# Strassen's seven products for both output projections of a two-layer encoder

## Chip, cores and metric

The kernel runs on one core of a Trainium2 chip. The metric is the device time of one execution in microseconds, as a median over runs of the same kernel. The core's engines are TensorE (PE, matmuls), VectorE (DVE), ScalarE (ACT), GpSimd (POOL) and SyncE (SP, which only issues DMAs here).

## What is computed

The encoder has two layers on 1024 tokens of width 1024. Layer 0 mixes tokens by neighbourhood attention, layer 1 by grouped-query attention with rotary positions. Around each mixer the reference does the same:

```python
for i in range(DEPTH):                       # DEPTH = 2
    h = rms_norm(x, norm_g[i])
    y = mixer(h, ...)                        # (o * silu(gate)) @ w_out is its last step
    x = x + y
    g = jax.nn.sigmoid(rms_norm(x, ple_norm_g[i]) @ ple_w_gate[i])
    x = x + g * (p[i] @ ple_w_proj[i])
return rms_norm(x, final_norm_g)
```

The change is in the product with `w_out`: (1024 x 1024) @ (1024 x 1024), once per layer.

## The kernel before

Each layer is a mixer (`mixer_a`, `mixer_b`) and then `dense_phase(l)`, which holds the output projection ("out") and the gate ("ple"). All products are done in about float32 precision with operands split in two: a high part, rounded to the matmul's type, and a low part, the rest. `split3` adds high by high, high by low and low by high into one PSUM bank, so every 128 x 128 by 128 x 512 product is three matmuls, recorded at line 315.

The left operand, the mixer's output, lies transposed in two resident tiles `HTh` and `HTl` (high and low; eight token tiles t of 128, eight contraction steps k of 128). During the mixer a head pair's output is split by `split` in `head_end` and stored to DRAM, and `load_y` brings it back into `HTh` and `HTl` near the mixer's end. The last pair (k = 7) is written by `fin_last` directly.

The right operand comes in units of 128 x 1024 floats (512 KB). The class `Weights` (`WQ`) goes through a list of units in order: `stage` loads a unit into one of two staging slots (`wstage`), `pump` splits it (high part on ACT at line 225, low part on DVE at line 230) into a pool with a limit of live units (`cap`), `get` forces it, `done` frees it, and `hold` names a unit at which loading stops. `pump` is called once after each piece of matmul work.

In `dense_phase` the projection's loops run over two halves of 512 output columns and eight token tiles, with eight k each: 16 groups of 24 matmuls, each in a PSUM bank of its own, added into the residual `X[t]` by DVE (line 1286). For the first four tiles all k below 4 come first. While the second half runs, finished tiles are normalised: ACT squares (lines 1360, 1369), `norm_r` with eleven small DVE instructions, a scaling on DVE (line 1382), and `to_ht` (PE transposes, ACT copy to `HTh` at 444, DVE rest to `HTl` at 445), placed three steps later between the projection's matmuls by `pend_ht`. The gate's two halves follow in the same way, with a tanh on ACT and two DVE instructions per tile (`gated`). In layer 0 `rope_tables`, which needs POOL, DVE and DMAs on SP, is run after tile 4 of the projection's first half.

Every engine takes its instructions in program order; the order between engines is set by semaphores. The program order is written out by hand.

## Time and profile before

| | us |
|---|---|
| median of 3 runs | 1548.74 |
| lowest, highest | 1548.33, 1549.39 |
| span of the profiled execution | 1548.4 |
| first matmul of the output projection, layer 0 and layer 1, from the start of the span | 529.28, 1355.76 |

The profile gives no time of its own for the profiled execution beside its span, first to last instruction; the span lies within the range of the runs. A row of a timeline reads: start, duration, engine, line, operation, output<-input, shapes, and in brackets how long the engine was idle before and which instruction ended that. A group's row reads: count, total busy time and mean ns of one, then the idle time before. PE's durations overlap, since matmuls are pipelined: the pitch from start to start is what counts.

### The profile page before, as it was taken

What the parts mean: (1) busy time and instruction counts of PE and PEld (TensorE: products, weight loads), DVE (VectorE), ACT (ScalarE), POOL (GpSimd) and SP (SyncE); (2) the same over time, 40 slices, a digit from 0 to 9 for tenths busy, and PEclk for the clock granted to TensorE, in tenths of its full rate; (3) what the DMA queues carried; (4) which work ended last, traced back from release to release, by engine and by line L of the source; (5) the groups of instructions that cost most, each with busy time, mean ns of one, the idle gap of its engine ahead of it and who ended that gap; (6) DMA issues with size and microseconds to landing.
All of it is one profiled execution on the core that took longest, in us unless ns stands there. A gap on an engine that the chain in (4) does not pass through costs nothing.

```text
span 1548.4 us, 24286 instructions
## 1 busy us (share of the span) xinstructions
PE 1521.1 (98%) x9072; PEld 1328.5 (86%) x9072; DVE 1016.2 (66%) x1990; ACT 874.1 (56%) x1757; POOL 280.4 (18%) x380
## 2 busy tenths in 40 slices
PE   8999999999999999999999999999999999999997
PEld 8888988988988888888988889989999888788886
DVE  7666576576477436557877776777777877625636
ACT  6565465465466522333567776767767767622422
POOL 1221121121121010000312122444131200000022
PEclk9999999999999999999999999999999999999999
DMA  8212122122033961232210111111101123651213
GB/s 263 97 40 72 60 80 61 52 82 79 35 99 97 355 232 55 79 139 78 75 48 22 38 48 50 41 38 56 57 27 42 62 62 116 224 197 55 74 54 131
DMA packets 90005, 138.32 MB, mean 89 GB/s; under 512 B 17056, under 2 KB 56096, under 8 KB 89888
## 3 DMA queue, kind: packets, MB, share of 16 engines
q1 hardware_dynamic: 87296, 129.17, 25.6%
q10 hardware_dynamic: 2592, 7.61, 1.4%
q8 instruction: 71, 1.16, 0.3%
q14 instruction: 46, 0.38, 0.1%
HBM read 104.13 MB, written 36.15 MB: 91 GB/s over the span
## 4 chain that ended last, share of the span: by engine, by line
PE 41%; DVE 7%; ACT 3%; issue 2%; DMA 0%; SPq 0%; ACTq 0%; DVEq 0%
PE d L315 22%; PE o L315 7%; PE t L1144 6%; PE s L315 5%; DVE PTl L1147 2%; DVE mn L1128 1%; ACT PTh L1146 1%; ACT P L1134 1%; PE t L443 1%; DVE QS L1108 1%; DVE wl L230 0%; PE t L1098 0%; DVE t L962 0%; DVE qt L963 0%; DVE Y L459 0%
## 5 line engine op out<-in xcount | busy, mean ns | idle before, releaser
L315 PE MATMUL d<-wh,HTh 128*128 128x256 f32 (+1 forms) x1096 | 369.3, 339 | 3.6 <-ACT HTh L444 1.3
L315 PE MATMUL d<-wh,HTl 128*128 128x256 f32 (+1 forms) x1096 | 363.2, 333 | 0.3 <-DVE HTl L445 0.3
L315 PE MATMUL d<-wl,HTh 128*128 128x256 f32 (+1 forms) x1096 | 362.6, 333 | 0.0
L1147 DVE TENSOR_TENSOR PTl<-t,PTh 128x512 fp32r<-128x512 f32 x256 | 164.4, 684 | 110.1 <-ACT PTh L1146 109.7
L315 PEld LDWEIGHTS d<-wh,HTh 128*128 128x128 f32 x1096 | 206.4, 189 | 26.6 <-ACT HTh L444 1.6
L315 PEld LDWEIGHTS d<-wl,HTh 128*128 128x128 f32 x1096 | 206.7, 189 | 21.7
L315 PEld LDWEIGHTS d<-wh,HTl 128*128 128x128 f32 x1096 | 206.5, 189 | 22.0 <-DVE HTl L445 0.5
L315 PE MATMUL d<-HTh,wh 128*128 128x512 f32 x504 | 205.8, 408 | 0.0
L315 PE MATMUL d<-HTh,wl 128*128 128x512 f32 x504 | 198.1, 393 | 0.0
L315 PE MATMUL d<-HTl,wh 128*128 128x512 f32 x504 | 197.5, 392 | 0.0
L1134 ACT ACTIVATE P<-s,mn 128x1024 f32<-128x1024 f32 x128 | 142.8, 1115 | 57.2 <-DVE mn L1128 56.3
L1146 ACT ACTIVATE PTh<-t 128x512 fp32r<-128x512 f32 x256 | 140.2, 594 | 45.4 <-PE t L1144 44.8
L1128 DVE TENSOR_REDUCE mn<-s 128x1 f32<-128x1024 f32 x128 | 154.8, 1209 | 11.7 <-PE s L315 11.6
L1144 PE MATMUL t<-ident,P 128*128 128x128 f32 x1024 | 137.7, 275 | 6.4 <-DVE PTl L1147 4.4
L230 DVE TENSOR_TENSOR wl<-wstage,wh 128x1024 fp32r<-128x1024 f32 x86 | 110.2, 1285 | 40.1 <-ACT wh L225 39.6
L1144 PEld LDWEIGHTS t<-ident,P 128*128 128x128 f32 x1024 | 114.6, 140 | 22.5 <-DVE PTl L1147 16.6
L315 PE MATMUL s<-KA,QS 128*128 128x512 f32 (+2 forms) x384 | 133.5, 402 | 0.0
L315 PE MATMUL s<-KB,QS 128*128 128x512 f32 (+2 forms) x384 | 121.7, 371 | 0.0
L315 PE MATMUL o<-PTh,V 128*128 128x256 f32 (+2 forms) x672 | 118.8, 288 | 1.2 <-DVE Y L459 0.9
L315 PE MATMUL o<-PTl,V 128*128 128x256 f32 (+2 forms) x672 | 119.0, 288 | 0.1
L695 DVE TENSOR_TENSOR PTl<-t,PTh 128x384 fp32r<-128x384 f32 (+1 forms) x128 | 66.6, 520 | 74.7 <-ACT PTh L694 73.4
L315 PEld LDWEIGHTS d<-HTh,wl 128*128 128x128 f32 x504 | 94.6, 188 | 21.7
(201 smaller groups left out, 2486.0 us busy)
## 6 DMA issues: line engine op xcount, KB each, us to landing
wstage<-in_wts SPq DMA_DIRECT2D x92, 512.0 KB
pp<-ppD SPq DMA_DIRECT2D x32, 256.0 KB
X<-in_x SPq DMA_DIRECT2D x15, 512.0 KB
rb<-rD SPq DMA_DIRECT2D x56, 128.0 KB
ppD<-th SPq DMA_DIRECT2D x20, 256.0 KB
xD<-X SPq DMA_DIRECT2D x8, 512.0 KB
X<-xD SPq DMA_DIRECT2D x8, 512.0 KB
yD0h<-rb SPq DMA_DIRECT2D x14, 256.0 KB
```

The costliest lines, as they stand in the source:

```text
L230: eng.tensor_tensor(lo[:, c:c + n], s[:, c:c + n], hi[:, c:c + n], ALU.subtract)
L315: pe.matmul(ps, a, b, start=first, stop=last, skip_group_check=True)
L443: pe.transpose(ps[:, k], xn[:, (4 * c + k) * 128:(4 * c + k + 1) * 128], ident)
L695: dve.tensor_tensor(PTl[:, sl], ps[:, :m], PTh[:, sl], ALU.subtract)
L1108: post.add(DQ, lambda: dve.tensor_tensor(qs[oth], raw[own], qs[own], ALU.subtract))
L1128: dve.tensor_reduce(mn, ps, axis=AX.X, op=ALU.min)
L1134: act.activation(p, ps, AF.Exp, bias=mn, scale=-1.0, accum_out=RS[h, hf][:, t:t + 1])
L1144: pe.transpose(ps[:, i], p[:, k * 128:(k + 1) * 128], ident)
L1146: act.activation(PTh[:, ks, c], ps, AF.Copy)
L1147: dve.tensor_tensor(PTl[:, ks, c], ps, PTh[:, ks, c], ALU.subtract)
```

## The change

Both operands of the projection are cut in halves: A (the mixer's output) by tokens and contraction into A11, A12, A21, A22, B (the weights) by contraction and columns. A quarter of A is four token tiles by four k. A block is one token tile of one product: four k, 12 matmuls into one bank. There are seven products of four blocks, in this order: A11 B11 (blocks 0 to 3), A12 B21 (4 to 7), S2 T2 (8 to 11), S3 T3 (12 to 15), A22 T4 (16 to 19), and, mixed, S1 T1 and Q4 B22 (20 to 27). The sums of A are S1 = A21 - A22, S2 = S1 - A11, S3 = A11 - A21, Q4 = S2 + A12; those of B are T3 = B22 + B12, T2 = T3 + B11, T4 = T2 + B21, T1 = B11 + B12. Products three to five and the last one add into the bank that an earlier product left (`start` False), after DVE's `fold` has read it.

The sums are made on chip while the blocks run. A dictionary `todo` gives each block a function that is issued after it. The sums of B need raw units in the staging slots and two more tiles (`sum0`, `sum1`); 14 raw units are loaded per layer beside the four that `WQ` splits, 18 where there were 8. DVE makes T3, POOL T2, T4 and T1; S1 and S2 are made by POOL for tiles 0, 2 and 3, by DVE for tile 1; S3 and Q4 by DVE. All sums are then split by ACT (high) and DVE (low), those of A back into `HTh` and `HTl`.

The mixers store A21's columns of the first four head pairs unsplit. The normalisation between projection and gate now squares whole rows on ACT, has its small instructions per pair of tiles (m, 4 + m), and the gate's first half goes through the tiles in the order 0, 4, 1, 5, 2, 6, 3, 7. The gate's weights are loaded only from block 20 on (`hold`). `rope_tables` comes after the last tile of the gate's first half.

```diff
-        for n in ("out", "ple"):
-            for hf in range(2):
-                q.extend([((n, l, hf, u), 1 + hf) for u in range(4)])
+        q.extend([(("out", l, 0, u), 1) for u in range(4)])
+        q.extend([(("ple", l, 0, u), 1) for u in range(4)])
+        q.extend([(("ple", l, 1, u), 4 - u // 2 * 2) for u in range(4)])
...
+    def strassen_out(l, X, ps_d, ps_t):
...
+        def halves(name, u, pid, src):
+            def hi():
+                if u == 0:
+                    W[name] = [None, None]
+                W[name][u] = WQ.alloc[pid]()
+                act.activation(W[name][u][0], src(), AF.Copy)
+
+            def lo():
+                w = W[name][u]
+                dve.tensor_tensor(w[1], src(), w[0], ALU.subtract)
+            return hi, lo
...
+        def s12(eng, m):
+            S1[m], S2[m] = piece("S1", 4), piece("S2", 2)
+            eng.tensor_tensor(S1[m], a21(m), h(4 + m, 1), ALU.subtract)
+            eng.tensor_tensor(S1[m], S1[m], lw(4 + m, 1), ALU.subtract)
+            eng.tensor_tensor(S2[m], S1[m], h(m, 0), ALU.subtract)
+            eng.tensor_tensor(S2[m], S2[m], lw(m, 0), ALU.subtract)
+
+        def s3(m):
+            S3[m] = piece("S3", 2)
+            dve.tensor_tensor(S3[m], h(m, 0), a21(m), ALU.subtract)
+            dve.tensor_tensor(S3[m], S3[m], lw(m, 0), ALU.add)
+
+        def q4(m):
+            Q4[m] = piece("Q4", 4)
+            dve.tensor_tensor(Q4[m], S2[m], h(m, 1), ALU.add)
+            dve.tensor_tensor(Q4[m], Q4[m], lw(m, 1), ALU.add)
...
+        def total(eng, u, dst, a, b):
+            eng.tensor_tensor(dst, a, b, ALU.add)
+
+        for u in range(2):
+            load(tc_[u], q22[u])
+            fetch(u, q12[u])
+        for t in range(2):
+            sync.dma_start(X[t], xs[t])
...
+        def f0():
+            s12(pool, 0)
+            for t in (2, 3):
+                sync.dma_start(X[t], xs[t])
+        at(0, f0)
+        def f1():
+            total(dve, 0, tc_[0], tc_[0], raw[0])
+            fetch(0, q11[0])
+            s3(0)
+        at(1, f1)
+        def f2():
+            total(dve, 1, tc_[1], tc_[1], raw[1])
+            fetch(1, q11[1])
+            s12(dve, 1)
+            s3(1)
+        at(2, f2)
+        def f3():
+            total(pool, 0, raw[0], raw[0], tc_[0])
+            hi_s(S2, 0)
+            hi_s(S3, 0)
+            lo_s(S2, 0)
+            lo_s(S3, 0)
+            q4(0)
+        at(3, f3)
+        def f4():
+            total(pool, 1, raw[1], raw[1], tc_[1])
+            hi_w("t3", 0)()
+            hi_s(S2, 1)
+            hi_s(S3, 1)
+            lo_s(S2, 1)
+            lo_s(S3, 1)
+        at(4, f4)
+        def f5():
+            s12(pool, 2)
+            lo_w("t3", 0)()
+            hi_w("t2", 0)()
+            q4(1)
+            for t in (4, 5):
+                sync.dma_start(X[t], xs[t])
+        at(5, f5)
+        def f6():
+            lo_w("t2", 0)()
+            hi_w("t2", 1)()
+            s3(2)
+        at(6, f6)
+        def f7():
+            s12(pool, 3)
+            lo_w("t2", 1)()
+            hi_w("t3", 1)()
+        at(7, f7)
+        def f8():
+            load(tc_[0], q21[0])
+            hi_s(S2, 2)
+            hi_s(S3, 2)
+            lo_w("t3", 1)()
+            lo_s(S2, 2)
+            lo_s(S3, 2)
+            s3(3)
+            for t in (6, 7):
+                sync.dma_start(X[t], xs[t])
+        at(8, f8)
+        def f9():
+            load(tc_[1], q21[1])
+            q4(2)
+            hi_s(S2, 3)
+            hi_s(S3, 3)
+            lo_s(S2, 3)
+            lo_s(S3, 3)
+        at(9, f9)
+        def f10():
+            total(pool, 0, tc_[0], tc_[0], raw[0])
+            q4(3)
+            fetch(0, q12[0])
+        at(10, f10)
+        def f11():
+            total(pool, 1, tc_[1], tc_[1], raw[1])
+            fetch(1, q12[1])
+        at(11, f11)
+        def first(m):
+            xt = X[m][:, 0:512]
+            pool.tensor_tensor(xt, xt, P1[m], ALU.add)
+        def f12():
+            hi_w("t4", 0)()
+            first(0)
+            first(1)
+        at(12, f12)
+        def f13():
+            lo_w("t4", 0)()
+            hi_w("t4", 1)()
+            load(tc_[0], q11[0])
+            first(2)
+            first(3)
+        at(13, f13)
...
+        def block(ps, t, c, wk, start):
+            for k in range(4):
+                wh, wl = W[wk][k // 2]
+                cc = slice((k % 2) * 512, (k % 2) * 512 + 512)
+                split3(ps, HTh[:, t, 4 * c + k, :], HTl[:, t, 4 * c + k, :], wh[:, cc], wl[:, cc],
+                       start and k == 0, k == 3)
+
+        def fold(t, c, ps, op):
+            xt = X[t][:, 512 * c:512 * c + 512]
+            if op is ALU.subtract:
+                dve.tensor_tensor(xt, xt, ps, op)
+            else:
+                dve.tensor_tensor(xt, ps, xt, op)
...
+        for wk, t0, c, xt0, xc, op in (("t2", 4, 0, 0, 1, ALU.subtract), ("t3", 0, 0, 4, 1, ALU.subtract),
+                                       ("t4", 4, 1, 4, 0, ALU.add)):
+            for m in range(4):
+                block(Y[m], t0 + m, c, wk, False)
+                fold(xt0 + m, xc, Y[m], op)
+                pulse()
+        WQ.live[1] += 2
+        WQ.live[2] += 2
+        for kind, m in ((5, 0), (5, 1), (3, 0), (5, 2), (3, 1), (5, 3), (3, 2), (3, 3)):
+            if kind == 5:
+                Y[m] = ps_d.tile([128, 512], F32, name="d")
+                block(Y[m], m, 1, "t1", True)
+                fold(4 + m, 1, Y[m], ALU.add)
+            else:
+                block(Y[m], 4 + m, 0, "b22", False)
+                fold(m, 1, Y[m], ALU.add)
+            pulse()
+            if clock[0] == 21:
+                es.close()
+            if (kind, m) == (5, 3):
+                WQ.live[1] -= 2
+            if (kind, m) == (3, 3):
+                WQ.live[2] -= 2
+            yield kind, m
...
+            for n, (step, m) in enumerate(strassen_out(l, X, ps_d, ps_t)):
...
+                if step == 5:
+                    act.activation(junk, X[4 + m], AF.Square, accum_out=ss[:, 2 * m + 1:2 * m + 2])
+                else:
+                    act.activation(junk, X[m], AF.Square, accum_out=ss[:, 2 * m:2 * m + 1])
+                    sm = ss[:, 2 * m:2 * m + 2]
+                    r = sb.tile([128, 2], F32, name="rn", bufs=4)
+                    wk = sb.tile([128, 8], F32, name="wkn", bufs=2)
+                    dve.tensor_scalar(sm, sm, 0.5 / D, 0.5 * EPS, op0=ALU.mult, op1=ALU.add)
+                    rsqrt(r, sm, wk)
+                    ready.append(((m, 4 + m), r))
+                WQ.pump()
+                pend_ht()
+                scale_pair()
```

More of the change, by code (lines that the diff above doesn't have):

```diff
@@ L256, in trunk @@
     WQ = Weights()
-    WQ.hold = ("bg", 0)
+    WQ.hold = ("ple", 0, 0, 0)
     q = WQ.q
@@ L530, in fin @@
             pool.tensor_tensor(Y, Y, rb, ALU.mult)
-            post.add(YS[layer], split)
+            if pair < 4 and hf == 1:
+                post.add(YS[layer] + 2, lambda: store(0, Y))
+            else:
+                post.add(YS[layer], split)
         return fin_last if pair == 7 else fin
@@ L1176, in mixer_b @@
                 if not pend:
-                    WQ.hold = None
+                    WQ.hold = ("ple", 1, 0, 0)
                 d[0]()
@@ L1263, in pend_ht, with scale_pair @@
                     to_ht(ps_t, *pend.pop(0)[1:])
-            for kind in ("out", "ple"):
-                final = kind == "ple" and l == 1
+            ready = []
+            def scale_pair():
+                if not ready or len(pend) > 4:
+                    return
+                ts, r = ready.pop(0)
+                xs = []
+                for i, t in enumerate(ts):
+                    xn = xalloc()
+                    dve.scalar_tensor_tensor(xn, X[t], r[:, i:i + 1], g1, op0=ALU.mult, op1=ALU.mult)
+                    xs.append(xn)
+                pend.extend([(clock[0] + 3, t, xn, (c,)) for c in range(2) for t, xn in zip(ts, xs)])
@@ L1267, in dense_phase @@
+            WQ.age, WQ.lag = age, lag
+            for kind in ("ple",):
+                final = l == 1
                 sq = sb.tile([128, 2, NT], F32, name="sq")
-                gt = g1 if kind == "out" else g2
+                gt = g2
                 for hf in range(2):
@@ L1329, in last_tile, with load_pp @@
                         WQ.done(*keys)
-                    def load_pp(t):
-                        if kind == "ple" and t < NT:
-                            PP[t] = sb.tile([128, 512], F32, name="pp")
-                            sync.dma_start(PP[t], ppD[l][t, :, cs])
-                    order = [(t, i) for t in range(NT) for i in range(2)]
-                    if kind == "out" and hf == 0:
-                        order = [(t, 0) for t in range(4)] + [(t, 1) for t in range(4)] + order[8:]
+                    def load_pp(i):
+                        if i < NT:
+                            PP[seq[i]] = sb.tile([128, 512], F32, name="pp")
+                            sync.dma_start(PP[seq[i]], ppD[l][seq[i], :, cs])
+                    order = [(t, i) for t in seq for i in range(2)]
+                    if hf == 0:
+                        order = [(t, i) for p in range(4) for i in range(2) for t in seq[2 * p:2 * p + 2]]
                     if final and hf == 1:
@@ L1342, in dense_phase @@
                     for t, i in order:
-                        if kind == "out" and hf == 0 and i == 0:
-                            sync.dma_start(X[t], xs[t])
                         if final and hf == 1 and t == NT - 1:
```

161 lines of the change are left out of this document (138 added, 23 removed).

## The prediction

> **What bounds the kernel now.** I read the page first, then the chain that ended last, then the windows around both output projections, then the timelines of PE, DVE, POOL and SP there and the groups by shape for durations.
>
> ```profile
> span 1548.4 us, 24286 instructions
> PE 1521.1 (98%) x9072; PEld 1328.5 (86%) x9072; DVE 1016.2 (66%) x1990; ACT 874.1 (56%) x1757; POOL 280.4 (18%) x380
> ...
> 1355.76 63.42 PE d L315 x276
> ```
>
> ```profile
> 536.00:587.00 51.00, 51.00 (x225) 41.90 (x224) 17.14 (x25) 13.05 (x26) 5.50 (x4) 1.00 0.65 219
> 1358.00:1415.00 57.00, 57.00 (x251) 46.85 (x250) 16.02 (x29) 12.99 (x26) 0.00 (x0) 1.00 0.40 148
> 595.00:635.00 40.00, 40.00 (x202) 32.77 (x201) 29.57 (x62) 14.72 (x29) 0.00 (x0) 1.00 0.19 57
> ```
>
> PE is busy for 98% of the span, and the chain that ended last runs through layer 1's output projection on PE alone, 63.42 us without a step to another engine. In the windows the columns are the stretch, its length, and the busy time of PE, PEld, DVE, ACT and POOL, then the granted clock, the DMA share and GB/s. In most of both output projections (first two rows) PE is never idle and DVE is busy for 17.1 of 51 and 16.0 of 57. So a matmul taken out there is worth its whole pitch. Where the projection turns into the gate (third row) PE is still full, but DVE is already at 29.6 of 40: there is little to spare there.
>
> ```profile
> 529.28 0.50 PE L315 MATMUL d<-wh,HTh 128*128 128x512 f32 x1 [0.74 <-ACT G L567]
> 532.15 0.39 PE L315 MATMUL d<-wh,HTh 128*128 128x512 f32 x1
> 532.83 0.39 PE L315 MATMUL d<-wh,HTh 128*128 128x512 f32 x1
> 1355.76 0.50 PE L315 MATMUL d<-wh,HTh 128*128 128x512 f32 x1 [0.73 <-ACT th L567]
> ```
>
> Between 532.15 and 532.83 lie three matmuls (high by high, high by low, low by high): one every 0.227 us, though each lasts 0.39. The first and last row are the first matmuls of the two projections; I count t from there.
>
> **Removed.** A projection has 8 token tiles x 8 contraction steps x 2 column halves x 3 = 384 matmuls. Seven products of 4 x 4 x 3 make 336. 48 x 0.227 = 10.9 us are saved per layer, 21.8 in all, if PE never waits. The splits of four head pairs' second half go too (4 ACT and 4 DVE instructions a layer), under the mixers' matmuls: nothing.
>
> **The clock of the new projection.** 28 blocks of 12 matmuls, 2.72 us each. Blocks 0 to 7 need only what is there today. Block 8 (due t = 21.8) needs S2 and T2 = B22+B12+B11, both units in high and low parts, and block 11 (due 29.9) needs S2 of the fourth token tile. So I follow DVE and POOL up to there. First, when do the raw weights arrive?
>
> ```profile
> 534.12 2.36 DVE L230 TENSOR_TENSOR wl<-wstage,wh 128x1024 fp32r<-128x1024 f32 x2
> 1357.81 2.44 DVE L230 TENSOR_TENSOR wl<-wstage,wh 128x1024 fp32r<-128x1024 f32 x2
> 535.40 0.33 SPq L208 DMA_DIRECT2D wstage<-in_wts  x1
> 538.91 1.06 ACT L225 ACTIVATE wh<-wstage 128x1024 fp32r<-128x1024 f32 x1 [4.48 <-DMA wstage<-in_wts]
> 536.00:545.00 9.00, 9.00 (x41) 7.48 (x40) 2.31 (x3) 1.06 (x1) 0.00 (x0) 1.00 0.96 328
> ```
>
> The two staging slots come free with the low parts of the last two units of B (first two rows): t = 3.3 and 4.5 in layer 1, 6.0 and 7.2 in layer 0. A load lands 3.5 us after issue (535.40 to 538.91), and behind it 512 KB at 328 GB/s take 1.6. In layer 1 the first B12 unit lands at 6.8, B22's second at 8.4, B12's second at 10.0, then X0 to X3, and B11's first unit, fetched after DVE's first sum but queued behind those X tiles, at about 18.
>
> ```profile
> 527.09 0.69 DVE L508 TENSOR_TENSOR Y<-Y,G 128x512 f32<-128x512 f32 x1
> 527.82 0.69 DVE L512 TENSOR_TENSOR Y<-Y,rb 128x512 f32<-128x512 f32 x1
> 533.51 0.69 DVE L516 TENSOR_TENSOR HTl<-Y,HTh 128x512 fp32r<-128x512 f32 x1 [0.70 <-ACT HTh L515]
> L530 POOL TENSOR_TENSOR Y<-Y,rb 128x512 f32<-128x512 f32 x28 | 36.5, 1304 | 141.4 <-DMA rb<-rD 140.9
> L529 POOL TENSOR_TENSOR Y<-Y,G 128x512 f32<-128x512 f32 x28 | 41.9, 1497 | 136.1 <-DVE Y L459 136.1
> L965 POOL TENSOR_TENSOR qt<-qt,t 128x256 f32<-128x256 f32 x24 | 18.2, 760 | 1.9
> ```
>
> On DVE 512 columns take 0.61 (533.51 to 534.12) when the next instruction is independent and 0.73 when it needs the result (527.09 to 527.82): 0.67 on average; 1024 columns 1.18 (2.36 for two). POOL needs 1.30 for 512 columns and 0.76 for 256, so an estimated 2.39 for 1024, which the trace does not show.
>
> From t = 10.0 DVE's own order up to the low part of T2's second unit holds 4 instructions of 1024 columns (second T3 sum, three low parts), 16 of 512 with both operands in SBUF (S1/S2 of tile 1, S3 of tiles 1 and 2, Q4 of tiles 0 and 1, four low parts) and 4 folds from PSUM: 4.7 + 10.7 + 2.4 = 17.9, t = 27.9. It was due at 23.1. Up to the low part of S2's fourth tile follow 1.2 + 7 x 0.67 + 2 x 0.61 = 7.1 and a wait of 0.9 for block 8's fold: 35.9, due at 30.4 (block 11's third matmul). DVE alone would make PE 5.5 us late in layer 1, and 2.7 more in layer 0, where the slots are free that much later: 8.2.
>
> **POOL and DVE at once.** In this stretch POOL adds beside DVE, and today's trace shows what that does.
>
> ```profile
> 304.36 3.45 DVE L230 TENSOR_TENSOR wl<-wstage,wh 128x1024 fp32r<-128x1024 f32 x2
> 304.41 2.32 POOL L529 TENSOR_TENSOR Y<-Y,G 128x512 f32<-128x512 f32 x1 [8.88 <-DVE Y L459]
> 1470.27 1.21 DVE L230 TENSOR_TENSOR wl<-wstage,wh 128x1024 fp32r<-128x1024 f32 x1
> 1470.54 2.10 POOL L1362 TENSOR_TENSOR X<-X,gain 128x512 f32<-128x512 f32 x1 [5.14 <-ACT xn L1360]
> 33.03 2.83 POOL L230 TENSOR_TENSOR wl<-wstage,wh 128x256 fp32r<-128x256 f32 x4 [18.75 <-ACT wh L225]
> 33.83 1.29 DVE L445 TENSOR_TENSOR HTl<-t,HTh 128x512 fp32r<-128x512 f32 x2
> ```
>
> In the timeline at 304 two DVE low parts took 3.45 instead of 2.36, and POOL's product begun 0.05 later took 2.32 instead of 1.30: first DVE, then POOL, then DVE again, nothing together. At 1470 POOL ends 1.2 after DVE did. At 33.8 two DVE subtractions that read PSUM keep their 1.29 beside POOL. So DVE instructions with both operands in SBUF take turns with POOL's, one for one; folds do not. The Trainium skill says the same (SBUF — State Buffer, "SBUF: two separate sides"): a DVE instruction with two SBUF inputs and a GpSimd instruction hold a shared port pair exclusively, each for its whole length. By that rule, too, the sum below stands, and the trace agrees with 2.32 and 3.45.
>
> From about t = 18 POOL's order up to that point is four sums of 1024 columns (T2, T4), S1/S2 of tiles 2 and 3 (8 x 1.30) and a first P1 addition: 9.6 + 10.4 + 1.3 = 21.3. Some 5 us of it lie beside six folds (3.7) and DVE's waits; 16.4 are pushed into DVE's order. S2's fourth low part comes at 35.9 + 16.4 = 52.3 instead of 30.4: PE is 21.9 late in layer 1, 24.6 in layer 0. If DVE always won, only what DVE and PE wait for would count (two sums and S1/S2, 15.2, less 3.7): 17.0 and 19.7. At L529's mean of 1.50 and the same stretch for sums it would be 3.5 more each. I take the turns that the rows show. Blocks 12 to 20 take 24.5: DVE has 6 low parts of weights, 8 of sums and 9 folds there (7.1 + 4.9 + 5.5 = 17.5), POOL 8.7 (three P1 additions, two T1 sums), and the folds run beside POOL: 17.5 + 8.7 - 5.5 = 20.7, no stall.
>
> **Where the projection turns into the gate.** Pairs of token tiles now finish at blocks 22, 24, 26 and 27, and block 27 adds into the bank that block 25's fold must first have read.
>
> ```profile
> 597.66 0.16 DVE L426 SCALAR_TENSOR_TENSOR stn<-sq 128x2 f32<-128x2 f32 x1
> 599.62 0.16 DVE L334 SCALAR_TENSOR_TENSOR stn<-wkn 128x2 f32<-128x2 f32 x1
> 599.82 2.48 DVE L1382 SCALAR_TENSOR_TENSOR xn<-X,stn,gain 128x1024 f32<-128x1024 f32 x2
> L736 ACT ACTIVATE junk<-X 128x1024 bf16<-128x1024 f32 x7 | 7.4, 1056 | 0.9 <-DMA X<-in_x 0.9
> 592.55 0.60 PE L443 MATMUL t<-ident,xn 128*128 128x128 f32 x4
> ```
>
> The first two rows are the first and last of the timeline's eleven small instructions: 2.16 to the start of the scaling. A square of 1024 columns is 1.06, with its accumulator read about 1.25, and DVE waits for it. From block 22's end: fold 0.8, square 1.25, small 2.16, two scalings 2.36, fold 0.6, low part of a gate weight 1.18, fold 0.6 (9.0); square 1.25, small 2.16, low part 1.18, scalings 2.36, and block 25's fold 0.7: 16.6. PE gets to block 27 after four blocks and two sets of transposes at 0.5 to 0.6: 11.9. It waits 4.7. Two low parts of the transposed input, which the gate's second and third block need, stand behind the next pairs. The first: square 1.25, gate weight's high part 1.06, copy 0.6, low part 0.6, fold 0.6, square 1.25, small 2.16, low part 1.18, low part 0.6 = 9.3, against two blocks, two sets of transposes and two matmuls, 6.9: 2.4 of waiting. The next: fold 0.6, square 1.25, small 2.16, low parts 1.18 and 0.6 = 5.8, against 3.2: 2.6. That is 9.7 per layer; it would be nothing if DVE found ACT's squares done each time, and one square (1.25) more if the gate weights' high parts come ahead of them.
>
> **Clock.**
>
> ```profile
> 1540.00:1542.00 2.00, 0.21 (x2) 0.01 (x1) 1.90 (x8) 1.73 (x3) 0.00 (x0) 1.00 0.00 0
> 1542.00:1544.00 2.00, 0.00 (x0) 0.00 (x0) 1.82 (x8) 1.68 (x4) 0.00 (x0) 0.90 0.05 16
> 1544.00:1546.00 2.00, 0.00 (x0) 0.00 (x0) 0.00 (x0) 0.00 (x0) 0.00 (x0) 0.50 1.00 399
> 1.34 1.97 PE L763 MATMUL gain<-ident 128*128 128x128 f32 x8 [1.34 <-POOL ident masks.py:199]
> ```
>
> After the last matmul (1540.2) the granted clock falls to 0.5 at about 1543.6, 3.4 us later. The long stalls (about 10, 5 and 5 us before blocks 8 and 11) exceed that. At the start of the run 128 columns take 0.22 each, twice what they take at 592.55. What a stall costs afterwards isn't in the trace; the bounds are nothing and about 3 us (the run's first 6 us at half speed). Most of it vanishes, since DVE is what PE waits for. Only after the last stall in front, before block 11, nothing absorbs it: taking for the recovery the 3.4 that the fall took (an estimate), at half speed, 1.7 per layer. The Trainium skill (TensorE: Matmul & The Clock Gate, "What's actually happening") gives about 3.4 us of sustained work before the clock is full again; by that alone the term would be the same 1.7.
>
> **Sum.** -21.8 + 24.6 + 21.9 + 2 x 9.7 + 2 x 1.7 = +47.5. The span 1548.4 lies 0.3 under the median of the runs, 1548.74, so what is around it is nothing that counts: 1596.
>
> The rope tables of layer 0 move to the end of the gate's first half: SP's queue holds them ahead of two pp loads. Their POOL work, four products of 512 columns, is 5.2 us; the three matmul blocks of lead that the transposes have cover it, and up to 5 us show if they don't.
>
> **Rivals.** *No exclusion.* If POOL's sums ran beside DVE's, only DVE's own load stays: -21.8 + 8.2 + 5.5 + 19.4 = +11.3, 1560. The pairs at 304 and 1470 speak against it; 12%.
> *PE never waits* (the other side). If DVE gets through its order before block 8's T2 is due, that is in 23.1 - 10.0 = 13.1 us instead of 17.9 and without POOL's turns, and the gate's start keeps up, the whole 10.9 per layer stays: 1527. For it: DVE was idle two thirds of the old projection. Against it: the work is not spread but due before block 8, and DVE is at three quarters where the gate begins. It turns into a loss once PE waits more than 10.9 per layer. 10%.
> *Slower still.* POOL at L529's mean, recovery of the clock at its bound and the rope tables in the open: 1596 + 7 + 2.6 + 5 = 1611 and over; 6%.
>
> **How the numbers follow.** My forecast has 72%, its own range 1586 (DVE always first at the port) to 1610. 1557 to 1610 takes in the first rival; left out are the 10% of the second and most of the last. About 0.2% is what a measurement of this kernel can tell from no change; stalls that just eat the gain, between the first two rivals, have 3% of the first one's 12. Faster 0.10, same 0.03, slower 0.87.
>
> **What would show it.** Right: 672 projection matmuls instead of 768; PE idle for some 15 us ahead of block 8, released by DVE low parts of T2, and again before block 11; DVE instructions of 512 columns at 1.5 to 2 us beside POOL's; a wait of 4 to 5 us before the last block, on a fold; granted clock under 1 in these places. Wrong: PE full through the projection; or POOL and DVE instructions overlapping at 1.30 and 0.69; or stalls ended by DMA instead of DVE.

## The result, and the profile after

The changed kernel took 1604.69 us (median of 4 runs, 1601.26 to 1609.34) against 1549.01 for the kernel before beside it (1548.33 to 1549.39): a ratio of 1.0361 (95% interval 1.0342 to 1.0380). The profiled execution took 1605.17 us, its span is 1603.3: 54.9 more than the span before.

The page of the changed kernel, its first lines and the clock in 40 slices:

```profile
span 1603.3 us, 24288 instructions
PE 1517.3 (95%) x8976; PEld 1323.8 (83%) x8976; DVE 1129.0 (70%) x2084; ACT 898.2 (56%) x1769; POOL 364.6 (23%) x424
...
PEclk9999999999999979999999999999999999979899
```

PE has 96 matmuls fewer (8976 instead of 9072), 48 in each projection, and is busy only 4 us less, though these were worth 21.8 at full clock: it waits, and where it has waited it runs at a low clock. The timeline of PE from the first matmul of each projection, with its waits of more than 1 us in brackets (first layer 0, then layer 1, each with the junction, the place where the projection turns into the gate):

```profile
528.89 0.50 PE L316 MATMUL d<-wh,HTh 128*128 128x512 f32 x1 [0.74 <-ACT G L571]
553.29 0.50 PE L316 MATMUL d<-wh,HTh 128*128 128x512 f32 x1 [2.33 <-ACT wh L1263]
566.60 0.80 PE L316 MATMUL d<-wl,HTh 128*128 128x512 f32 x1 [12.80 <-DVE wl L1267]
573.26 0.80 PE L316 MATMUL d<-wl,HTh 128*128 128x512 f32 x1 [3.73 <-DVE wl L1267]
585.89 0.79 PE L316 MATMUL d<-wh,HTl 128*128 128x512 f32 x1 [2.66 <-DVE HTl L1305]
636.74 0.66 PE L316 MATMUL d<-wh,HTh 128*128 128x512 f32 x1 [5.05 <-DVE X L1509]
651.61 0.50 PE L316 MATMUL d<-wh,HTl 128*128 128x512 f32 x1 [2.28 <-DVE HTl L446]
720.21 1.08 PE L444 MATMUL t<-ident,xn 128*128 128x128 f32 x4 [6.05 <-DVE xn L1739]
...
1389.54 0.50 PE L316 MATMUL d<-wh,HTh 128*128 128x512 f32 x1 [0.74 <-ACT th L571]
1422.78 0.79 PE L316 MATMUL d<-wl,HTh 128*128 128x512 f32 x1 [10.96 <-DVE wl L1267]
1428.36 0.79 PE L316 MATMUL d<-wl,HTh 128*128 128x512 f32 x1 [2.65 <-DVE wl L1267]
1440.99 0.50 PE L316 MATMUL d<-wh,HTl 128*128 128x512 f32 x1 [3.49 <-DVE HTl L1305]
1491.94 0.79 PE L316 MATMUL d<-wh,HTh 128*128 128x512 f32 x1 [5.05 <-DVE X L1509]
1506.82 0.50 PE L316 MATMUL d<-wh,HTl 128*128 128x512 f32 x1 [2.22 <-DVE HTl L446]
```

The waits stand where T2's parts (its first high part, L1263, in layer 0 for 2.33, then DVE's low parts, L1267, one wait per unit) and the low part of S2's fourth tile (L1305) are late, in blocks 8 and 11; the one before block 27 is for a fold (L1509), those of 2.2 to 2.3 behind it are for a low part of the gate's input (L446); the one at 720 belongs to the rope tables. To put a length on each part I mark four points: the first projection matmul, the last wait in front, the eighth tanh of the gate (the end of its first half) and the last tanh. The eighth tanh on ACT, before (L1278) and after (L1641), both layers:

```profile
668.81 0.60 ACT L1278 ACTIVATE th<-d 128x512 f32<-128x512 f32 x1 [2.58 <-PE d L315]
1495.28 0.60 ACT L1278 ACTIVATE th<-d 128x512 f32<-128x512 f32 x1 [2.57 <-PE d L315]
```

```profile
694.82 0.58 ACT L1641 ACTIVATE th<-d 128x512 f32<-128x512 f32 x1
1551.59 0.58 ACT L1641 ACTIVATE th<-d 128x512 f32<-128x512 f32 x1
```

From the first projection matmul to the eighth tanh it was 139.5 in both layers and is now 165.9 and 162.05: +26.4 and +22.5. From there to the last tanh of the gate it was 48.7 and 45.0 and is 57.0 and 43.8: +8.3 and -1.2. That makes 56.0; all the rest of the span gives 1.1 back.

Why DVE is late: DVE and POOL in the same stretch of the timeline, then one POOL sum that began ahead of the DVE instruction beside it.

```profile
549.85 2.85 DVE L1298 TENSOR_TENSOR Q<-S,HTh 128x512 f32<-128x512 f32 x1
552.73 2.72 DVE L1299 TENSOR_TENSOR Q<-Q,HTl 128x512 f32<-128x512 f32 x1
555.38 0.68 DVE L1509 TENSOR_TENSOR X<-t,X 128x512 f32<-128x512 f32 x1
...
549.62 5.28 POOL L1320 TENSOR_TENSOR wstage<-wstage,sum 128x1024 f32<-128x1024 f32 x2 [8.56 <-DMA wstage<-in_wts]
556.66 1.59 POOL L1287 TENSOR_TENSOR S<-S,HTl 128x512 f32<-128x512 f32 x1
...
1436.35 2.37 POOL L1320 TENSOR_TENSOR sum<-sum,wstage 128x1024 f32<-128x1024 f32 x1 [5.82 <-DMA sum<-in_wts]
1436.48 2.78 DVE L1299 TENSOR_TENSOR Q<-Q,HTl 128x512 f32<-128x512 f32 x1
```

Two additions of 512 columns, 0.69 each when alone, take 2.85 and 2.72 beside POOL's two sums of 1024: one POOL sum lies inside each. The fold at 555.38 reads PSUM and keeps its 0.68. The POOL sum at 1436.35 began 0.13 ahead of a DVE addition and took 2.37 (the estimate for an undisturbed one was 2.39); the DVE addition took 2.78 instead of 0.69. So the one that comes first keeps its time and the other waits for it.

### The profile page after: what moved, and what is told of

The parts are those of the page before. It is cut to its first block, busy times and chain, and to the rows that moved or that the text cites. A ratio compares the mean times of both kernels' runs of the same rounds, so it can differ in the third digit from the quotient of the medians.

```text
span 1603.3 us, 24288 instructions
## 1 busy us (share of the span) xinstructions
PE 1517.3 (95%) x8976; PEld 1323.8 (83%) x8976; DVE 1129.0 (70%) x2084; ACT 898.2 (56%) x1769; POOL 364.6 (23%) x424
## 5 line engine op out<-in xcount | busy, mean ns | idle before, releaser
L316 PE MATMUL d<-wl,HTh 128*128 128x256 f32 (+1 forms) x1032 | 344.4, 336 | 30.1 <-DVE wl L1267 30.1
L316 PE MATMUL d<-wh,HTh 128*128 128x256 f32 (+1 forms) x1032 | 350.6, 342 | 15.3 <-DVE X L1509 10.1
L316 PE MATMUL d<-wh,HTl 128*128 128x256 f32 (+1 forms) x1032 | 344.5, 336 | 11.4 <-DVE HTl L1305 6.2
L316 PEld LDWEIGHTS d<-wl,HTh 128*128 128x128 f32 x1032 | 199.0, 194 | 51.6 <-DVE wl L1267 32.3
L316 PEld LDWEIGHTS d<-wh,HTh 128*128 128x128 f32 x1032 | 198.6, 193 | 37.0 <-DVE X L1509 10.6
L316 PEld LDWEIGHTS d<-wh,HTl 128*128 128x128 f32 x1032 | 198.9, 194 | 32.8 <-DVE HTl L1305 7.0
L1148 PEld LDWEIGHTS t<-ident,P 128*128 128x128 f32 x1024 | 114.7, 140 | 21.3 <-DVE PTl L1151 15.6
L230 DVE TENSOR_TENSOR wl<-wstage,wh 128x1024 fp32r<-128x1024 f32 x78 | 101.4, 1305 | 29.3 <-ACT wh L225 28.8
```

What stands on the lines that cost most here:

```text
L230: eng.tensor_tensor(lo[:, c:c + n], s[:, c:c + n], hi[:, c:c + n], ALU.subtract)
L316: pe.matmul(ps, a, b, start=first, stop=last, skip_group_check=True)
L1148: pe.transpose(ps[:, i], p[:, k * 128:(k + 1) * 128], ident)
```

## The experiments

Each is compared with the changed kernel (1604.7) or with the kernel before, run beside it on the same chip (1549.6 to 1550.6).

**e1: rope tables two tiles earlier.**

```diff
-                        if l == 0 and hf == 0 and t == seq[-1]:
-                            rope_tables(sb)
                         load_pp(seq.index(t) + 2)
+                        if l == 0 and hf == 0 and t == seq[5]:
+                            rope_tables(sb)
```

> The rope tables of layer 0 are built at the sixth token tile of the gate's first half instead of the eighth, behind that tile's pp load. Theory: the 6.05 us stall at 720 and the low clock behind it come from the tables' loads and stores, which stand in SP's queue ahead of two pp loads; two tiles (10.9 us) earlier they are done when the pp buffers come free. The stall goes, about -8 us: 1596 (1593 to 1600). Rival: the pp loads would be late anyway, because the front's lateness shifted DVE's work into this place, or POOL's four products slow DVE there: no change, 1602 to 1606, or the stall only moves.

1601.64 us (1600.22 to 1603.77): -3, a little over a third of what was expected. The wait at 720 is gone, but new ones came. DVE and PE of e1:

```profile
692.04 1.74 DVE L1757 TENSOR_SCALAR xn<-xn 128x1024 f32<-128x1024 f32 x1 [7.05 <-POOL xn L1754]
...
694.43 0.71 PE L316 MATMUL d<-wh,HTl 128*128 128x512 f32 x1 [2.57 <-DVE HTl L446]
```

DVE's scaling of the products waits 7.05 for POOL, and a low part that PE needs is queued behind it; the eighth tanh, counted from the first projection matmul, comes 2.7 later than in the changed kernel. In layer 0 the stretch from the first projection matmul to the last tanh is 6.1 shorter, not 8.3; elsewhere the profiled run is 2.6 longer, within the scatter of these runs. Looking back at the changed kernel, the queues are seen (SP, POOL, DVE):

```profile
704.00 2.96 SPq L1759 DMA_DIRECT2D ropeD<-xn  x4
707.01 5.74 SPq L1693 DMA_DIRECT2D pp<-ppD  x3
...
699.65 5.48 POOL L1754 TENSOR_TENSOR xn<-xn,th 128x512 f32<-128x512 f32 x4 [93.84 <-DMA xn<-in_rope]
...
702.21 1.76 DVE L1757 TENSOR_SCALAR xn<-xn 128x1024 f32<-128x1024 f32 x1 [5.37 <-POOL xn L1754]
711.72 0.69 DVE L1642 SCALAR_TENSOR_TENSOR th<-th,pp 128x512 f32<-128x512 f32 x1 [4.37 <-DMA pp<-ppD]
```

SP holds the stores until POOL and DVE are done (704.00), the pp loads start at 707.01, and the gate's product waits for them.

**e5: rope tables in three parts.** Loads, products and stores one tile apart (`rope_tables` now yields after its loads and after its products), and the gains scaled instead of the products:

```diff
+                        if l == 0 and hf == 0 and t in seq[4:7]:
+                            if t == seq[4]:
+                                rope = rope_tables(sb)
+                            next(rope, None)
...
-            if kind == 0:
-                dve.tensor_scalar(ro, ro, -0.125, None, op0=ALU.mult)
+        dve.tensor_scalar(hg[:, :128], hg[:, :128], -0.125, None, op0=ALU.mult)
```

> The rope tables of layer 0 in three parts over the gate's first half: loads behind the fifth tile, POOL's four products behind the sixth, stores behind the seventh, each behind that tile's pp load; the head gains get a tile of their own instead of one that the tanh results use, and DVE scales 128 columns of the gains ahead of the products instead of 1024 of the products. Theory: what the tables cost is only the waits in order behind them (SP's pp loads, DVE's scaling that waits for POOL, the tanh tile that POOL holds): with none of them in the way the gate's second half of layer 0 takes what it took before, -8 us, 1595 to 1599. Rival (POOL's products slow DVE at the port, or PE is late in this place anyhow): 2 to 3 us stay, 1600 and over.

1595.76 us (1594.67 to 1601.18), -8.9. The gate's second half in layer 0 is 48.26, as before the change (48.70), with POOL's four products still there (5.03). So the 8.3 were waits in order behind the tables, not their work. (The profiled run is the slowest of the four: up to the eighth tanh it is 1.7 and 1.5 longer than the changed kernel, which the edit doesn't touch.)

**e2: S1/S2 of tiles 2 and 3 on DVE.**

```diff
-            s12(pool, 2)
+            s12(dve, 2)
...
-            s12(pool, 3)
+            s12(dve, 3)
```

> S1/S2 of token tiles 2 and 3 (8 instructions of 512 columns a layer) are made on DVE instead of POOL. Theory (DVE and POOL take turns at one port, so what counts is the sum of both): -8 x 1.30 for POOL, + 8 x 0.67 for DVE of which a part was already covered by folds and waits; block 12 moves by less than 2 us per layer, the time stays within 4 us of the changed kernel, 1598 to 1606. Rival 1 (no exclusion, DVE alone is late): DVE gets 8 x 0.67 = 5.4 us more per layer, +10.7, 1615. Rival 2 (POOL alone is the long pole): 10.4 us less per layer, -21, 1583.

1603.82 us (1602.49 to 1606.79), no change. PE's last wait in front ends 56.4 and 52.7 after the first matmul (57.0 and 51.45 in the changed kernel). Eight instructions that took POOL 1.6 to 2.1 each in this stretch, and take DVE 0.72 in e2, can change engines and little moves. The rows say why: beside one of these POOL additions a DVE instruction was 0.5 to 1.1 longer (1.68 instead of 1.22 for 1024 columns, 1.76 instead of 0.69 for 512), so DVE pays about the same whether it waits for the addition or makes it. What counts here is what both engines do together. Both rivals (+10.7 and -21) fall.

**e3: without POOL's sums.**

```diff
-            s12(pool, 2)
+            S1[2], S2[2] = S1[0], S2[0]
...
-            total(pool, 0, raw[0], raw[0], tc_[0])
...
-            total(pool, 0, tc_[0], tc_[0], raw[0])
```

> Leaves out POOL's S1/S2 of token tiles 2 and 3 (those of tiles 0 and 1 are used in their place) and POOL's sums for T2 and T4 (weights without them are used); DVE, ACT, PE and the loads do all that they did. Theory (turns at the port): what is left in front is DVE's own load: block 12 about 11 us late in layer 0 and 8 in layer 1 instead of 28.3 and 22.8, so -30 to -35 us in all: 1569 to 1574. Rival (DVE's load or the loads of weights decide, POOL is unimportant): within 5 us of the changed kernel.

1581.01 us (1580.30 to 1581.55): -23.7, less than the 30 to 35 that were expected. Its last wait in front in each layer, then one of the additions that POOL still makes there and the DVE instruction beside it:

```profile
575.80 0.50 PE L316 MATMUL d<-wh,HTl 128*128 128x512 f32 x1 [1.08 <-DVE HTl L1305]
...
1419.11 0.50 PE L316 MATMUL d<-wh,HTl 128*128 128x512 f32 x1 [0.41 <-DVE HTl L1305]
...
558.08 2.12 POOL L1426 TENSOR_TENSOR X<-X,P 128x512 f32<-128x512 f32 x1 [1.28 <-DVE X L1505]
559.00 1.75 DVE L1298 TENSOR_TENSOR Q<-S,HTh 128x512 f32<-128x512 f32 x1
```

The first matmuls stand at 531.95 and 1377.96 in this run, so the last wait ends 43.85 and 41.15 after them: 13.15 and 10.3 sooner. Taking POOL's sums away wins back about half of the lateness, 23.5 of 48. What stays is not all DVE alone: POOL's four additions of P1 now come forward into this stretch (1.59 to 2.14 each), and three DVE instructions ahead of T2's last low part are 1.1 longer beside them (559.00 is one), 3.2 per layer. Counting these in, the turns with POOL come to as much as 16.4 and 13.5.

**e6: PE kept busy ahead of block 8.**

```diff
             for m in range(4):
+                if wk == "t2" and m == 0:
+                    ps = ps_t.tile([128, 4, 128], F32, name="t").rearrange("p k c -> p (k c)")
+                    for i in range(60 if l == 0 else 44):
+                        mm(ps, HTh[:, 7, 4], HTh[:, 7, 4:8].rearrange("p k c -> p (k c)"), True, True)
                 block(Y[m], t0 + m, c, wk, False)
```

> Ahead of block 8 PE makes 60 (layer 0) and 44 (layer 1) matmuls of 512 columns whose result is not used, which fill the long wait there. Theory (DVE releases blocks 8 and 11, the clock costs only after the last wait): blocks 8 to 11 run at full clock, but block 11 waits for DVE as before; block 12 comes earlier by 0 to 2 us per layer: 1600 to 1605, and the granted clock in these windows is near 1. Rival 1 (the low clock is a large part of the lateness): 4 us or more per layer, 1597 or less. Rival 2 (the chip's clock falls later for the work added): no gain or slower.

1606.73 us (1604.12 to 1608.81): no gain, and just above the expected range. PE of e6, then its windows (stretch, length, busy time of PE, PEld, DVE, ACT, POOL, granted clock, DMA share, GB/s):

```profile
556.08 16.07 PE L316 MATMUL t<-HTh 128*128 128x512 f32 x60 [5.14 <-DVE X L1509]
584.00 0.50 PE L316 MATMUL d<-wh,HTl 128*128 128x512 f32 x1 [3.22 <-DVE HTl L1305]
```

```profile
555.00:560.00 5.00, 3.92 (x9) 3.15 (x10) 5.00 (x6) 1.91 (x2) 4.78 (x3) 0.50 0.02 3
560.00:565.00 5.00, 5.00 (x22) 4.08 (x21) 4.96 (x5) 0.00 (x0) 4.91 (x3) 0.92 0.59 189
585.00:590.00 5.00, 5.00 (x17) 4.00 (x16) 4.60 (x5) 1.68 (x4) 5.00 (x4) 0.69 0.21 82
```

In layer 0 the extra matmuls had to wait for a bank and ran past the time at which T2's first unit was ready (566.60 in the changed kernel, where block 8 had begun at 553.29 and then waited). Block 8 began at 571.99, and PE ran at full clock from there to the wait before block 11's third matmul. That wait ends 55.1 after the first matmul instead of 57.0, but kernels with the same front and no extra matmuls (e1, e4, e5, e9) end it between 55.1 and 57.1. DVE waits 1.54 for block 8's fold instead of 2.60: about 1 us of the low clock does reach DVE. The rest of it is hidden, because block 11 waits for DVE in both. In layer 1 the 44 matmuls were over at 1422.4 and T2's second unit was ready only at 1428.9, so PE waited 4.53 again and the clock fell; the last wait ends 54.2 after the first matmul instead of 51.45. There the edit did not keep the clock up, and the question is answered by layer 0 alone. The eighth tanh came after 165.6 and 163.2 (165.9 and 162.05 in the changed kernel). The wait before block 11 lowers the clock again (0.69): that loss e6 did not take away. The second rival's reason doesn't show: the mean granted clock over the span is 0.984 to 0.988, against 0.974 to 0.980 in the changed kernel.

**e4: late statistics.** The eleven small DVE instructions and the scaling one block later (`late` makes the statistics of the pair before, behind this block's fold):

```diff
+                late()
                 if step == 5:
...
-                    dve.tensor_scalar(sm, sm, 0.5 / D, 0.5 * EPS, op0=ALU.mult, op1=ALU.add)
-                    rsqrt(r, sm, wk)
-                    ready.append(((m, 4 + m), r))
+                    dl.append(m)
```

> The eleven small DVE instructions and the scaling of a pair of token tiles are issued one block later, behind the next block's fold (from the last pair on as before). Theory: PE's 5.05 us before block 27 come from the fold of block 25, which stands on DVE behind a square that DVE waits for; it goes. The scaled tiles come later for it, so the gate's first blocks wait about 2 more at two places: net -1 to -3 per layer, 1598 to 1602. Rival 1 (the wait is paid once and nothing else is late): -5 per layer, 1594. Rival 2 (DVE's sum of work up to the gate decides, the order does not): the 5 us appear in full at the gate's start, no change.

1603.41 us (1600.08 to 1603.71), a little above the expected 1598 to 1602. Of the 5.05 before block 27 nothing is left in layer 0 and 1.80 in layer 1, and this stands in layer 0's gate, in its first block, instead (4.37 in layer 1):

```profile
637.23 0.80 PE L316 MATMUL d<-wh,HTh 128*128 128x512 f32 x1 [4.34 <-ACT HTh L445]
```

The stretch up to the eighth tanh is 3.2 shorter in layer 0 and 0.3 in layer 1; the medians differ by less than the runs scatter. The wait names ACT: its copy of a transposed tile stands behind a square, which waits for a fold, which stands behind DVE's scaling.

**e9: copies ahead of the squares**, with e4 and e5:

```diff
+                pend_ht()
                 late()
...
                 WQ.pump()
-                pend_ht()
                 scale_pair()
```

> The changed kernel with the spread rope tables (e5), the late statistics (e4) and, in the junction, the transposes with ACT's copies ahead of the next square on ACT; the projection's front as it was. Theory (in e4 the wait moved to ACT's copy behind a square that waits for a fold behind DVE's scaling): 3 to 4 us less per layer than e4's order, with e5's 9 off: 1586 to 1592; the front's 28 and 23 us stay. Rival (DVE's amount of work decides in the junction): as e5 with e4's 1 to 3, 1592 to 1597.

1587.23 us (1585.16 to 1588.31), 8.5 below e5. The stretch up to the eighth tanh is 160.7 and 158.45: 5.2 and 3.6 less than in the changed kernel, while the last wait in front ends 57.1 and 51.5 after the first matmul, as there (57.0 and 51.45). Nearly half of the junction's cost was the order of the instructions.

**e7: weight sums ahead, in layer 0's mixer.** With e4 and e5:

```diff
+            for ci, (l, u, c) in enumerate([(l, u, c) for l in range(2) for u in range(2) for c in range(4)]):
+                chunk(l, u, c, 2 + 7 * ci)
...
+        def weights(name):
+            for u in range(2):
+                w = WQ.alloc[pid[name]]()
+                for dst, src in zip(w, tD[name, l, u]):
+                    sync.dma_start(dst.bitcast(F32), src)
...
-        for wk, t0, c, xt0, xc, op in (("t2", 4, 0, 0, 1, ALU.subtract), ("t3", 0, 0, 4, 1, ALU.subtract),
-                                       ("t4", 4, 1, 4, 0, ALU.add)):
+        for wk, t0, xt0 in (("b21", 0, 0), ("t4", 4, 4)):
```

chunk() spreads one piece of 256 columns over eight steps of the mixer: loads, the sums, their high and low parts, stores to tD. Blocks of t2 and t3 follow those of t4, S1 to S3 are all made by DVE, and POOL has nothing to do in the projection.

> All weight sums of both layers (T1 to T4, and B22) are made during layer 0's mixer in pieces of 256 columns, split in high and low parts there on ACT and DVE and kept in DRAM; the projection loads the parts and has no weight arithmetic for them. S1 to S3 all on DVE; A22T4 (which needs no sum of tokens) is moved ahead of S2T2, into a bank of its own, for which DVE has 4 more folds; P1 is added to X by DVE from PSUM, POOL does nothing in the projection. The late statistics of e4 and the spread rope tables of e5 are in it. Theory (DVE and POOL work due before blocks 8 and 11 is the cause of the front's lateness): from block 0 to block 20 PE waits 0 to 3 us per layer instead of 28 and 23; the junction keeps 6 to 9 per layer; the mixer takes 50 us more of DVE and 25 of ACT beside PE at up to 3 us: 1541 to 1552. Rival 1 (the mixer's chain has no room for DVE's additional work): 10 us or more later at the first projection, 1555 and over. Rival 2 (the loads, not the sums, set the front): waits ended by DMA, 1565 and over.

1590.20 us (1586.69 to 1592.29), far above the expected 1541 to 1552. In front PE does not wait at all in either layer, and the eighth tanh comes after 136.6 and 137.6: 2.9 and 1.9 sooner than in the kernel before. Several things changed at once for this: the weight sums are gone, POOL is idle, and T2 and S2 are due four blocks later; which of them freed the front is not shown. But the first projection starts at 572.53, 43.3 later than before. From the waits of e7 and of e8 up to there (us in total, times, longest):

```profile
PE t L697 <- ACT sp L689: 33.9, 31, 4.9
...
ACT wh L887 <- DMA tDt301h<-wh: 6.7, 1, 6.7
```

```profile
PE t L697 <- ACT sp L689: 20.9, 25, 1.7
```

In the mixer PE's transposes wait for the exponential on ACT, in e7 up to 4.9 at a time; ACT's own wait of 6.7 is for a high tile that a store still reads.

**e8: less of it, more tiles.** T1's split and B22 go back into the projection, three high tiles of their own:

```diff
-          for n in ("b22", "t3", "t1", "t2", "t4") for l in range(2) for u in range(2)}
+          for n in ("t3", "t1", "t2", "t4") for l in range(2) for u in range(2)}
...
-                    high("wh0", "wd")
+                       7: [low("wh1", "wc"), high("wh2", "wd")], 8: [store("t2", "wc", "wh1"), low("wh2", "wd")],
```

> As e7, with half of the waiting taken out of the mixer: T1 is only summed there and B22 not touched (both are split in the projection's second half, where DVE had idle time in e7), each piece has three high tiles of its own instead of two that are used again after 8 us, and DVE gets at most two of the added instructions per step. In the junction the transposes and ACT's copies of a scaled tile go ahead of the next square on ACT. Theory (e7's 43 us in the mixer are waits in ACT's and SP's order for tiles that a store still reads, not the amount of added work; and the front is free once its sums are gone): first projection 0 to 8 us later than before instead of 43; no wait of PE in front; from the first projection matmul to the eighth tanh 133 to 135 instead of 139.5: 1537 to 1548. Rival 1 (the amount of DVE work in the mixer counts: e7's 50 us, here 36): 25 us or more late, 1558 and over. Rival 2 (T1 and B22 split in the projection bring waits back before blocks 20 to 27): 5 us more per layer, 1550.

1562.43 us (1561.99 to 1563.01). The waits for stores are gone, but the first projection is still 25.7 late (first matmul at 554.95). The front is free of waits all the same, and with e9's order the eighth tanh comes after 134.0 and 134.6. By the number this is rival 1, that DVE's amount of work in the mixer counts; e10 decides.

**e10: the same work behind the scores.**

```diff
-                    for f in todo.pop(n, ()):
-                        att.append((f, 0.0))
...
                         def scores(n=n):
                             f_S(*steps[n + 2])
+                            for f in todo.pop(n, ()):
+                                f()
```

> As e8, but in the mixer the added work of each step is issued behind the next scores' DVE instruction (it stood ahead of it) and without steps of its own in the list that paces the staging of weights and the gates' late parts. Theory (e8's 25.7 us in the mixer are 25 waits of PE's transposes for the exponential, which the added DVE and ACT instructions stand ahead of; behind them they fall into time in which DVE waits for ACT): first projection 0 to 8 us later than before, 1537 to 1545. Rival (DVE's and ACT's amount of work in the mixer counts, wherever it stands): 20 us or more late, 1556 and over.

1540.86 us (1537.97 to 1541.74) against 1550.56: a ratio of 0.9936 (0.9920 to 0.9953). It beats both kernels, by 9.7 us (0.6%, clear of the interval) and about 64 us, and rival 1 falls: the added work is that of e8. Its wait in the mixer, its first matmuls and eighth tanhs, and the windows of both projections:

```profile
PE t L697 <- ACT sp L689: 1.9, 5, 0.8
```

```profile
533.63 0.50 PE L318 MATMUL d<-wh,HTh 128*128 128x512 f32 x1 [0.74 <-ACT G L573]
667.88 0.58 ACT L1546 ACTIVATE th<-d 128x512 f32<-128x512 f32 x1
1353.03 0.50 PE L318 MATMUL d<-wh,HTh 128*128 128x512 f32 x1 [0.74 <-ACT th L573]
1487.53 0.58 ACT L1546 ACTIVATE th<-d 128x512 f32<-128x512 f32 x1
```

```profile
535.00:590.00 55.00, 55.00 (x245) 45.53 (x244) 52.09 (x79) 15.11 (x23) 0.00 (x0) 1.00 0.60 235
1355.00:1410.00 55.00, 55.00 (x244) 45.58 (x243) 49.86 (x76) 13.63 (x20) 0.00 (x0) 1.00 0.58 228
```

PE is full, DVE is at 52 and 50 of 55, POOL does nothing. The mixer costs 4.35, the two projections with the gate's first half gain 5.3 and 5.0, the rest 3.2. Two things differ from e8 in the mixer, the place of the added instructions and that they no longer count as steps for what is paced by steps; which of them gave how much of the 21 us was not taken apart.

## Why the prediction was right

The forecast was 1596.0 and slower, in a range of 1557 to 1610; it came to 1604.7, by the mechanism named in front; where the projection turns into the gate the sum came out partly by luck, and the rope tables' term failed. Term by term, in the profiled execution:

| term | predicted | measured |
|---|---|---|
| matmuls taken out | -21.8 | -21.8 (672, at 0.227) |
| front, up to the last wait before block 11, layer 0 / 1 | 24.6 / 21.9 | 26.6 / 21.05 |
| low clock behind it, per layer | 1.7 | about 1.6 |
| junction, layer 0 / 1 | 9.7 / 9.7 | 9.1 / 10.8 (what is left) |
| rope tables | 0 (up to 5) | 8.3 |
| gate's second half, layer 1, and the rest | 0 | -1.2, -1.1 |

The front is the end of the last wait (585.89 and 1440.99) less the first matmul and less the 30.4 at which block 11's third matmul was due. The clock: in these rows of the changed kernel three matmuls take 1.28 (0.43 each) from 586.48 to 587.76, and 0.69 (0.23 each) again from 589.78:

```profile
586.48 0.63 PE L316 MATMUL d<-wh,HTh 128*128 128x512 f32 x1
587.76 0.63 PE L316 MATMUL d<-wh,HTh 128*128 128x512 f32 x1
589.78 0.40 PE L316 MATMUL d<-wh,HTh 128*128 128x512 f32 x1
590.47 0.40 PE L316 MATMUL d<-wh,HTh 128*128 128x512 f32 x1
```

Some 3.2 us at half speed cost 1.6, as estimated; in layer 1 the half clock came 1.5 after the wait and lasted 3.4, from 1442.49 to 1445.90, and cost the same. The Trainium skill's 3.4 us of sustained work (TensorE: Matmul & The Clock Gate, "What's actually happening") fits here. That the low clock in blocks 8 to 10 is hidden behind DVE holds but for about 1 us, by e6's layer 0.

The junction is what is left of +26.4 and +22.5 after the terms above it, and its parts did not come as predicted. The long wait, on the fold of block 25, was 5.05 in both layers (predicted 4.7). The gate's second block waited 0.42 in layer 0 and not at all in layer 1 (predicted 2.4), the third 2.28 and 2.22 (predicted 2.6). In place of what is missing stands a low clock that the prediction put at nothing here, since it counted only the one behind the last wait in front:

```profile
641.18 0.60 PE L444 MATMUL t<-ident,xn 128*128 128x128 f32 x4
```

Block 27 takes from 636.74 to these transposes, 4.44, and 5.22 in layer 1; the gate's next block takes 2.8. In layer 1 the block behind the 2.22 is slowed as well, by some 1.7. That the junction's sum still came near 9.7 is luck.

The step that failed is the rope tables'. The clause "the three matmul blocks of lead that the transposes have cover it" priced POOL's 5.2 us of work; the queues were named (two pp loads behind the stores on SP) and then not walked. The first store waits for POOL's products and DVE's scaling until 704.00, the pp loads follow at 707.01, and the product that needs the first of them starts at 711.72. e5 leaves the work in and removes the waits: -8.9.

Inside the front term the parts held better than e3 alone would say. In the changed kernel's own rows, from the second T3 sum to the low part of S2's fourth tile, DVE's instructions are 15.3 and 13.3 longer in sum than the same ones undisturbed (0.69 or 1.22 each); POOL's turns were put at 16.4. The second T3 sum starts at t = 14.5 and 11.0 instead of 12.7 and 10.0: in layer 0 DVE waited for the first weight unit until 11.7, in layer 1 its first sum took 2.35 beside POOL. And DVE waits 2.6 for block 8's fold instead of 0.9. In part these differences cancel: the term came out within 2.0 and 0.85, its largest part within 1.1 and 3.1.

Of the rivals, "no exclusion" falls with the rows at 549 to 557 and with e2: on that theory e2 adds 10.7. The Trainium skill's rule on the port (SBUF — State Buffer, "SBUF: two separate sides") agrees with the 2.85 beside POOL and the 0.68 of the fold. "PE never waits" is what e10 reaches in front, by other means, and even so it keeps 5.3 and 5.0 of the 10.9 per layer; two waits in its junction (1.83 and 1.94 in layer 0) take a part of the rest, and what takes the remainder was not measured. Of the three conditions of "slower still" one came true, the rope tables in the open (8.3, more than its 5); the turns with POOL and the clock behind the front's last wait stayed at or under their estimates. (Its price for POOL at L529's mean, 3.5 per layer, should be 3.2 by its own figures, 21.3 x 1.497 / 1.304; nothing hangs on it.)

## What to carry to other kernels

A product saved on a full PE is worth its pitch only if its sums are not due at once: price the additions of DVE and POOL together, as one queue when both work on operands in SBUF, up to the first block that needs them, and make those that depend on weights alone long before. When work is moved, walk every in-order queue that it joins (SP's loads behind its stores, DVE behind its wait for POOL, ACT behind a copy), since e5, e9 (against e5) and e10 (against e8) moved instructions and hardly added any, and won 8.9, 8.5 and some 21 us; in e10 the pacing had changed too. A stall that an experiment removes can come back one queue further: look for the next wait before crediting the fix.

## What the runs showed of the hardware that was not expected

The changed kernel scatters by 8.1 us between its runs, e5 by 6.5, e7 by 5.6; the kernel before by 1.1 to 3.7, e8 by 1.0 and e10 by 3.8. Long waits of PE alone do not explain it: e1, e3, e4 and e9 have them too and scatter by 3.6, 1.3, 3.6 and 3.2. The mean granted clock over the span is 0.974 to 0.980 in the changed kernel's four runs, and the longest, 1609.34, has the lowest. What decides it stays open.

The time that PE needs to come back to full clock is not set by the length of the wait. By the pitch of its matmuls it ran at half clock for about 3.2 us behind the wait of 2.66 (from 585.89), 5.6 behind the one of 3.73 (from 573.26), and 3.6 and 5.1 behind the two of 5.05 (from 636.74 and 1491.94). In e6 it was some 4.7, with work that never paused: 60 matmuls took 16.07 instead of 13.6, with 0.50 granted from their start at 556.08 up to 560 and 0.92 from 560 to 565. So the Trainium skill's 3.4 (TensorE: Matmul & The Clock Gate, "What's actually happening") is not what every wait costs, and the measurement decides. A wait of 2.28 in layer 0 (651.61) left the clock full, one of 2.22 in layer 1 (1506.82) was followed by half clock.
